# One root chain, modulation ahead of weight splits, and third-tile products one group later in the opening of a two-layer decoder step

## Chip, cores and metric

The kernel runs on one NeuronCore of one Trainium2 chip. The metric is the device time of one execution in microseconds; the times are medians of several executions.

## The reference

One inference step of a two-layer decoder for 512 prompt tokens and 8 sample tokens that share all weights (520 columns in all, width 1024). Each layer computes a modulated norm, a mixer, a gated residual, a second modulated norm, a convolutional feed-forward net and another gated residual. What matters here is the way into the first mixer:

```python
mod = (silu(c) @ w_ada[l] + b_ada[l])[:, None, :]        # c: 1 prompt row, 8 sample rows
sh1, sc1, g1, sh2, sc2, g2 = split(mod, 6, axis=-1)
h = x * rsqrt(mean(x * x, -1, keepdims=True) + 1e-6) * (1 + sc1) + sh1
z = h @ w_in                                             # layer 0: u, v_a, q, k, v
```

Everything is float32.

## The kernel before

Activations lie with the width on the partitions: X is 8 tiles (k = 0 to 7) of 128 partitions and 520 tokens. Every large product is made of three passes in a rounded float32 format: a weight tile W is split into a high part wh (ScalarE, L228) and a low part wl = W - wh (VectorE, L229), the activation h into HH and HL, and the output sums wh·HH, wh·HL and wl·HH. The helper `mm3` issues these three, each for two column ranges (256 and 264), so one weight tile and one k cost six matmuls (rows of L267).

Instructions are issued in the order of the program, each engine's queue in that order; a tile's readers wait for its writers through semaphores. Weight tiles come in the fixed order `stream` (first a query, a key and a value tile of the first mixer) through three raw buffers on SyncE's queue; `issue_load` starts a transfer, `issue_split` makes wh and wl of the next tile, and `weights()` hands out the next pair, splitting it if that is still to be done, and creates background tasks that run at later ticks of `proj`.

The opening (L1205 on) computes the first modulated norm and the first three weight tiles together. The adaLN shift and scale of layer 0 are made in four groups of two k each (`START`), by the generator `h_start(g)`, which `step(g)` moves on to its next `yield`:

- first call: the products of adaLN tiles k = 0 to 3 (L359, 32 matmuls, "ada"); their weights are 8 transfers of 256 KB for a group, issued by `ada_load_start` (L344);
- second call: those of k = 4 to 7, and the evacuation to `adae` on ScalarE (L365);
- third call: the fold product `adat` (L368), which brings shift and scale onto the partitions; then VectorE adds the bias ("mod"), and for each of the group's two tiles makes nt = X·(1 + scale)·rsb; ScalarE makes HH = nt + shift (L1239), VectorE HL = (nt + shift) - HH (L95); some short instructions do the sample columns.

`rsb` holds the reciprocal root of each token's mean square on all partitions. It comes from `rstd_half`, run once for each half of the tokens: sum products with a column of ones (L468), square root on ScalarE (L469), reciprocal on VectorE (L472), a broadcast transpose on TensorE (L477) and a copy (L1256).

The three accumulators are `trip`: query and key in two wide PSUM tiles ("mm"), the value tile in two narrow ones ("tr"). `part(i, k)` is the six matmuls of tile i and k; `qk_part(k)` is those of tiles 0 and 1, a pair; `v_part(g)` is tile 2 for the two k of group g. What sets the order is the list of calls that the diff shows: before, pair 0, then for each group its adaLN halves with pairs between, the fold product, and third-tile products. After the three tiles comes `mixer_even`, whose first product is the next value tile.

Two matmuls on zeros (`warm2`, L1263) stand ahead of pair 0.

Of the kernel before, what the change touches and what calls it, by code (L numbers as in the profile page):

```python
# [8 lines left out]
F32 = mybir.dt.float32  # L9
F32R = mybir.dt.float32r  # L10
AF = mybir.ActivationFunctionType
ALU = mybir.AluOpType
# [3 lines left out]
D = 1024  # L16
KD = 8
TP = 512
NS = 8
T = TP + NS  # L20
# [9 lines left out]
HALF = ((0, H0), (H0, T))  # L30
# [20 lines left out]
def kernel(ctx: ExitStack, tc: tile.TileContext, I: dict, O: dict):  # L51
    nc = tc.nc
    cp = ctx.enter_context(tc.tile_pool(name="cp", bufs=1))
# [20 lines left out]
    def nm(s):  # L74
        uid[0] += 1
        return f"{s}_{uid[0]}"

    def slot(s, dt=F32):
        return bp.tile([128, T], dt, name=nm(s), tag="b")

    def bank(s="ps"):
        return psum["ps"].tile([128, 512], F32, name=nm(s), tag="ps")
# [7 lines left out]
    act, vec, pool, pe = nc.scalar, nc.vector, nc.gpsimd, nc.tensor  # L90
# [3 lines left out]
    def stt(out, in0, s, in1, op0, op1):  # L94
        vec.scalar_tensor_tensor(out, in0, s, in1, op0=op0, op1=op1)  # L95
# [9 lines left out]
    def spawn(gen, delay=0):  # L105
        t = Task(gen, delay)
        tasks.append(t)
        return t
# [35 lines left out]
    ident = cp.tile([128, 128], F32, name="ident")  # L144
    ones = cp.tile([128, 1], F32, name="ones")
    eps = cp.tile([128, 1], F32, name="eps")
# [56 lines left out]
    def issue_load():  # L203
        i = pos["ld"]
        if i >= len(stream):
            return
        ap, n = src(stream[i])
        t = wp.tile([128, 1024], F32, name=nm("wr"), tag="wr", bufs=RBUFS)
        ld(t[:, :n * 128], ap)
        W[i] = (t, n)  # L210
        pos["ld"] += 1
        if stream[i][0] in ("up", "down") and i % 2 == 0 and pos["cp"] < len(copies):
            o, s = copies[pos["cp"]]
            ld(o, s)
            pos["cp"] += 1

    def issue_split():
        i = pos["sp"]
        if i >= len(stream):
            return  # L220
        t, n = W.pop(i)
        if stream[i][0] == "gates":
            h, l = (wp.tile([128, 1024], F32R, name=nm("wa"), tag="wa", bufs=4) for _ in range(2))
        else:
            h = wp.tile([128, 1024], F32R, name=nm("wh"), tag="wh", bufs=WBUFS)
            l = wp.tile([128, 1024], F32R, name=nm("wl"), tag="wl", bufs=WBUFS)
        w = n * 128
        act.activation(h[:, :w], t[:, :w], AF.Copy)  # L228
        vec.tensor_tensor(l[:, :w], t[:, :w], h[:, :w].bitcast(F32), op=ALU.subtract)  # L229
        SPLIT[i] = (h, l)  # L230
        pos["sp"] += 1

    def split_task(i):
        yield 1
        fill_loads()
        while i >= pos["rel"] + WBUFS or pos["sp"] < i or (stream[i][0] == "gates" and not ada_rest.done):
            yield 1
        if pos["sp"] <= i:
            issue_split()
        fill_loads()  # L240
# [5 lines left out]
    def used(n):  # L246
        pos["rel"] += n

    def weights():
        i = pos["use"]  # L250
        while pos["ld"] <= i:
            issue_load()
        while pos["sp"] <= i:
            issue_split()
        pos["use"] += 1
        pos["plan"] = max(pos["plan"], pos["sp"])
        while pos["plan"] <= min(i + SPLIT_AHEAD, len(stream) - 1):
            spawn(split_task(pos["plan"]))
            pos["plan"] += 1
        return SPLIT.pop(i)  # L260
# [92 lines left out]
    def ada_start(g):  # L353
        ts = ada_q.pop(0)
        js, n = START[g], len(START[g])
        ps = bank("ada")
        for k in range(KD):
            for c in range(2 * n):
                pe.matmul(ps[32 * c:32 * c + 32, 0:128], cpad[:, k, :], ts[k][:, 128 * c:128 * c + 128],  # L359
                          start=k == 0, stop=k == KD - 1)  # L360
            if k == 3:
                yield
        r = 64 * n
        ev = sp.tile([128, 512], F32, name=nm("adae"), tag="adae", bufs=1)
        act.activation(ev[0:r, 0:128], ps[0:r, 0:128], AF.Copy)  # L365
        yield
        pt = bank("adat")
        pe.matmul(pt[:, 0:18 * n], ev[0:r, 0:128], fold[0:r, 0:18 * n], start=True, stop=True)  # L368
        ptv = pt[:, 0:18 * n].rearrange("p (c r) -> p c r", c=2 * n)
        for v in (1, 0):  # L370
            s = slice(js[0], js[-1] + 1)
            mod_add(MOD[0][:, v, s, :], ptv[:, v * n:v * n + n, :], 0, v, s)
# [67 lines left out]
    ssq_t = {}  # L440

    def ssq(k, t0=0, t1=T):

        ssq_add()
        if k == 0:
            ssq_t["t"] = slot("ssq")
        t = ssq_t["t"]
        q = t if k == 0 else slot("sq")
        act.activation(q[:, t0:t1], X[:, k, t0:t1], AF.Square)  # L449
        if k:  # L450
            ssq_t["late"] = (t[:, t0:t1], q[:, t0:t1])

    def ssq_add():
        late = ssq_t.pop("late", None)
        if late is not None:
            vec.tensor_tensor(late[0], late[0], late[1], op=ALU.add)

    def rstd_half(half, d1, d2, work=None):

        t = ssq_t["t"]  # L460
        ssq_add()
        yield d1
        ps = bank("ssq")
        starts = [HALF[half][0], HALF[half][0] + 128] + ([T - 128] if half else [])
        n = len(starts)
        sd = sp.tile([128, 4], F32, name=nm("sd"), tag="sd")
        for c, o in enumerate(starts):
            pe.matmul(ps[:, c:c + 1], t[:, o:o + 128], ones, start=True, stop=True)  # L468
        act.activation(sd[:, 0:n], ps[:, 0:n], AF.Sqrt, bias=eps, scale=1.0 / D)  # L469
        if work is not None:  # L470
            work()
        vec.reciprocal(sd[:, 0:n], sd[:, 0:n])  # L472
        yield d2
        rb = bank("rb")
        for c, o in enumerate(starts):
            o -= HALF[half][0]
            pe.transpose(rb[:, o:o + 128], sd[:, c:c + 1].to_broadcast([128, 128]), ident)  # L477
        return rb
# [738 lines left out]
    act_preload(AF.Sqrt)  # L1217
    for k in range(KD):
        ssq(k)

    def run(gen):
        try:
            while True:
                next(gen)
        except StopIteration as e:
            return e.value

    rsb = slot("rsb")

    def h_start(g):  # L1230
        yield from ada_start(g)
        js = slice(START[g][0], START[g][-1] + 1)
        t8 = h_sample_scale(0, 0, js)
        M, c = MOD[0], slice(0, TP)
        ts = []
        for n, k in enumerate(START[g]):
            t = slot("nt")
            stt(t[:, c], X[:, k, c], M[:, 1, k, 0:1], rsb[:, c], ALU.mult, ALU.mult)
            act.activation(HH[:, k, c], t[:, c], AF.Identity, bias=M[:, 0, k, 0:1])  # L1239
            if n == 0:  # L1240
                low = h_sample(0, 0, t8, rsb[:, 256:T], js)
            ts.append((k, t))
        for n, (k, t) in enumerate(ts):
            stt(HL[:, k, c], t[:, c], M[:, 0, k, 0:1], HH[:, k, c].bitcast(F32), ALU.add, ALU.subtract)
            if n == 0:
                low()
# [3 lines left out]
    def step(g):  # L1250
        next(hs[g], None)

    step(0)
    for h, (a, b) in enumerate(HALF):
        r = run(rstd_half(h, 0, 0))
        vec.tensor_copy(rsb[:, a:b], r[:, 0:b - a])  # L1256
    ws = [weights()]
    step(0)
    ws.append(weights())
    step(0)  # L1260
    wps = bank("warm2")
    for _ in range(2):
        pe.matmul(wps, warm[:, 0:128], warm, start=True, stop=True)  # L1263
# [3 lines left out]
    def part(i, k):  # L1267
        mm3(regs[i], ws[i][0], ws[i][1], k, Hs[0][k], Hs[1][k], k == 0, k == KD - 1)

    def qk_part(k):  # L1270
        part(0, k)
        part(1, k)

    def v_part(g):
        part(2, 2 * g)
        part(2, 2 * g + 1)

    qk_part(0)
    ada_load_start(3)
    step(1)  # L1280
    qk_part(1)
    ws.append(weights())
    step(1)
    step(1)
    v_part(0)
    for g in (1, 2):
        step(g + 1)
        qk_part(2 * g)
        step(g + 1)
        qk_part(2 * g + 1)  # L1290
        if g == 2:
            ld(pk[:, PACK["b_ada"][1]:], I["pack"][:, PACK["b_ada"][1]:])
            for _ in range(2):
                issue_load()
        step(g + 1)
        v_part(g)
    issue_split()
    for k in (6, 7):
        qk_part(k)
        part(2, k)  # L1300
    used(3)

    def norm_of(l, which):
# [7 lines left out]
    t = mixer_even(trip_regions, norm_of(0, 1))  # L1311
# [7 lines left out]
    t = ffn(0, after(t), norm_of(1, 0), gate_weights)  # L1319
    t = mixer_odd(after(t), norm_of(1, 1))  # L1320
# [24 lines left out]
    t = ffn(1, after(t), final)  # L1345
    finish(t)
    while pos["cp"] < len(copies):
        o, s = copies[pos["cp"]]
# [128 lines left out]
```

## Time and profile before

| | |
|---|---|
| time, median of 3 runs | 1279.53 us (1277.06 to 1281.1) |
| profiled execution | 1275.57 us |
| its span, first to last instruction | 1273.8 us |
| mean granted TensorE clock | 0.989 |
| TensorE matmul busy | 1236.5 us, 97% |
| VectorE, ScalarE, GpSimd busy | 56%, 45%, 6% |

The times of the trace count from the start of the span. PE is TensorE, DVE is VectorE, ACT is ScalarE, SPq the queue of SyncE that issues transfers. A matmul's end is modelled, so one row may overlap the next. "Idle before" is the time that the engine stood still ahead of an instruction, with what ended it.

### The profile page before, as it was taken

Reading aid. Unit: us, or ns where it says so; the run is one execution under the profiler, and the core shown is the slowest. Engines: PE = TensorE matmul, PEld = TensorE weight load, DVE = VectorE, ACT = ScalarE, POOL = GpSimd, SP = SyncE. Lnnn points to the kernel's source line nnn. Section 1 sums busy time; section 2 is a strip of 40 time slices with the busy share of each in tenths; the row PEclk is TensorE's granted clock in tenths of the full one; section 3 lists DMA queues with packets and bytes.
Section 4 is the critical chain, followed back from the end, with each engine's and each line's share of the span. In section 5 each row is a group of like instructions: output and inputs, shape, how many; then the busy total and the mean of one; then the engine's idle time right before and its main releaser. Section 6 shows DMA issues by size and latency. Waiting matters only on the chain.

```text
span 1273.8 us, 24556 instructions
## 1 busy us (share of the span) xinstructions
PE 1236.5 (97%) x10395; PEld 1159.0 (91%) x10395; DVE 717.7 (56%) x1385; ACT 577.4 (45%) x1002; POOL 79.8 (6%) x143
## 2 busy tenths in 40 slices
PE   8999999999999999999999898999999999999997
PEld 5888767798999999999999898998999999999996
DVE  5646557457743555425664877656655555445544
ACT  4434453235531444214453577734642454225434
POOL 0111322201011000010000000000000000000000
PEclk8999999999999999999999999999999999999998
DMA  9643676755688676775454222245447455545322
GB/s 359 246 162 120 206 249 211 271 182 201 240 275 313 232 261 250 259 255 197 151 204 149 84 84 69 61 142 180 149 162 252 149 199 182 199 153 195 120 81 75
DMA packets 54990, 239.76 MB, mean 188 GB/s; under 512 B 7504, under 2 KB 10328, under 8 KB 53856
## 3 DMA queue, kind: packets, MB, share of 16 engines
q1 hardware_dynamic: 36976, 177.37, 40.3%
q0 software_dynamic: 16816, 59.75, 13.5%
q8 instruction: 82, 1.34, 0.4%
q10 hardware_dynamic: 1088, 1.07, 0.3%
q14 instruction: 28, 0.23, 0.1%
HBM read 232.92 MB, written 72.31 MB: 240 GB/s over the span
## 4 chain that ended last, share of the span: by engine, by line
PE 83%; DVE 5%; ACT 5%; issue 4%; DMA 2%; POOL 1%; SPq 0%; DVEq 0%; POOLq 0%; ACTq 0%
PE mm L267 70%; PE half L267 5%; PE ada L421 2%; ACT wh L228 1%; DVE wl L229 1%; DMA wa<-in_wada 1%; DVE nt L95 1%; DVE HL L95 1%; PE pv L749 1%; PE qk L716 1%; PE ada L388 1%; PE pt L737 1%; DMA X<-in_xT 1%; PE ss L814 0%; DMA wr<-in_w 0%
## 5 line engine op out<-in xcount | busy, mean ns | idle before, releaser
L267 PE MATMUL mm<-HH,wh 128*128 128x256 f32 (+1 forms) x1968 | 420.6, 289 | 7.6 <-DVE X L531 7.3
L267 PE MATMUL mm<-HL,wh 128*128 128x256 f32 (+1 forms) x1968 | 411.5, 284 | 0.7 <-DVE HL L95 0.3
L267 PE MATMUL mm<-HH,wl 128*128 128x256 f32 (+1 forms) x1968 | 409.6, 283 | 0.0
L267 PEld LDWEIGHTS mm<-HH,wh 128*128 128x128 f32 x1968 | 310.7, 189 | 35.8 <-issue 21.2
L267 PEld LDWEIGHTS mm<-HL,wh 128*128 128x128 f32 x1968 | 311.6, 189 | 2.3 <-DVE HL L95 1.9
L267 PEld LDWEIGHTS mm<-HH,wl 128*128 128x128 f32 x1968 | 311.7, 189 | 0.0
L229 DVE TENSOR_TENSOR wl<-wr,wh 128x1024 fp32r<-128x1024 f32 (+1 forms) x188 | 224.3, 1199 | 78.1 <-ACT wh L228 77.1
L228 ACT ACTIVATE wh<-wr 128x1024 fp32r<-128x1024 f32 (+1 forms) x188 | 193.2, 1036 | 111.7 <-PE mm L267 103.5
L95 DVE SCALAR_TENSOR_TENSOR fy<-fraw,pk,fy 128x511 f32<-128x511 f32 (+1 forms) x176 | 132.1, 751 | 190.8 <-ACT fy L604 187.7
L603 ACT ACTIVATE fraw<-mm 128x520 f32<-128x520 f32 x88 | 53.2, 604 | 212.6 <-PE mm L267 212.6
L267 PE MATMUL mm<-gh,wh 128*128 128x256 f32 x576 | 116.8, 284 | 0.0
L267 PE MATMUL mm<-gh,wl 128*128 128x256 f32 x576 | 115.9, 283 | 0.0
L267 PE MATMUL mm<-gl,wh 128*128 128x256 f32 x576 | 115.9, 283 | 0.0
L267 PEld LDWEIGHTS mm<-gh,wh 128*128 128x128 f32 x576 | 89.2, 188 | 7.5 <-issue 7.5
L267 PEld LDWEIGHTS mm<-gh,wl 128*128 128x128 f32 x576 | 89.3, 188 | 0.0
L267 PEld LDWEIGHTS mm<-gl,wh 128*128 128x128 f32 x576 | 89.3, 188 | 0.0
L528 DVE TENSOR_TENSOR r<-mm,mod 128x8 f32<-128x8 f32 x48 | 8.0, 167 | 125.7 <-PE mm L267 125.7
L604 ACT ACTIVATE fy<-mm,pk 128x520 f32<-128x520 f32 x88 | 68.7, 781 | 0.0
L583 ACT ACTIVATE gh<-fs 128x520 fp32r<-128x520 f32 x44 | 28.1, 639 | 81.3 <-DVE fs L621 81.3
L376 POOL DMA_DIRECT2D wa<-in_wada x80 | 42.4, 533 | 335.0 <-PE ada L421 221.9
L449 ACT ACTIVATE sq<-X 128x520 f32<-128x520 f32 (+2 forms) x51 | 25.1, 501 | 76.1 <-DVE X L531 52.9
L584 DVE TENSOR_TENSOR gl<-fs,gh 128x520 fp32r<-128x520 f32 x44 | 30.8, 701 | 30.4 <-ACT gh L583 30.3
(280 smaller groups left out, 1473.5 us busy)
## 6 DMA issues: line engine op xcount, KB each, us to landing
wr<-in_w SPq DMA_DIRECT2D x140, 512.0 KB, 3.7
wa<-in_wada POOLq DMA_DIRECT2D x80, 512.0 KB, 5.7
wr<-in_wd SPq DMA_DIRECT2D x32, 512.0 KB, 3.7
wa<-in_wada SPq DMA_DIRECT2D x32, 256.0 KB, 5.4
out_ck<-in_ck SPq DMA_DIRECT2D x8, 1022.0 KB, 6.6
out_cv<-in_cv SPq DMA_DIRECT2D x8, 1022.0 KB, 6.3
sg<-in_kg POOLq DMA_DIRECT2D x16, 384.0 KB, 4.1
sg<-in_vg POOLq DMA_DIRECT2D x12, 512.0 KB, 5.3
```

Source lines behind the costliest of these rows:

```text
L95: vec.scalar_tensor_tensor(out, in0, s, in1, op0=op0, op1=op1)
L228: act.activation(h[:, :w], t[:, :w], AF.Copy)
L229: vec.tensor_tensor(l[:, :w], t[:, :w], h[:, :w].bitcast(F32), op=ALU.subtract)
L267: pe.matmul(o, w[:, c], x[:, t], start=start and n == 0, stop=stop and n == 2)
L376: st(t, I["wada"][n, k])
L388: pe.matmul(ps[32 * c:32 * c + 32, 0:256], cpad[:, k, :], t[:, 256 * c:256 * c + 256], start=k == 0, stop=k == KD - 1)
L421: pe.matmul(ps[c:c + 32, :], cpad[:, k, :], t[:, 512 * h:512 * h + 512], start=k == 0, stop=k == KD - 1)
L449: act.activation(q[:, t0:t1], X[:, k, t0:t1], AF.Square)
L583: act.activation(h, v, AF.Copy)
L584: vec.tensor_tensor(l, v, h.bitcast(F32), op=ALU.subtract)
L603: act.activation(raw, whole(ps), AF.Copy)
L604: act.activation(y, whole(ps), AF.Identity, bias=b[:, f:f + 1], scale=w[:, 2, f:f + 1])
```

## The change

Four edits, all in the opening:

- The sums of squares of all tokens go through one square root (`sd0`, five columns of 128 tokens) and one reciprocal, then five transposes, one copy of 512 columns and one of 8, in place of two chains over halves. The sum products stand between the two halves of group 0's adaLN products, the transposes behind the second half.
- For group 0, `h_start` has one more `yield` between HH and HL. The first weight's high part is issued ahead of the fold product's modulation, its low part (`q_low`) between HH and HL; the second weight's split follows HL.
- The third weight is taken (`ws.append(weights())`) after group 1's modulation in place of before it.
- The loop now runs over groups n = 1 to 3 (g = n - 1 in the code): first adaLN half of group n, from n = 2 on the third-tile products of group n - 2, pair 2n - 1, second adaLN half, fold product and modulation, pair 2n. The third-tile products of groups 2 and 3 and pair 7 follow the loop.

```diff
--- before.py
+++ after.py
@@ -214,7 +214,10 @@
             ld(o, s)
             pos["cp"] += 1
 
-    def issue_split():
+    def low(t, h, l, w):
+        vec.tensor_tensor(l[:, :w], t[:, :w], h[:, :w].bitcast(F32), op=ALU.subtract)
+
+    def issue_split(low_later=False):
         i = pos["sp"]
         if i >= len(stream):
             return
@@ -226,9 +229,11 @@
             l = wp.tile([128, 1024], F32R, name=nm("wl"), tag="wl", bufs=WBUFS)
         w = n * 128
         act.activation(h[:, :w], t[:, :w], AF.Copy)
-        vec.tensor_tensor(l[:, :w], t[:, :w], h[:, :w].bitcast(F32), op=ALU.subtract)
         SPLIT[i] = (h, l)
         pos["sp"] += 1
+        if low_later:
+            return lambda: low(t, h, l, w)
+        low(t, h, l, w)
 
     def split_task(i):
         yield 1
@@ -1217,13 +1222,9 @@
     act_preload(AF.Sqrt)
     for k in range(KD):
         ssq(k)
-
-    def run(gen):
-        try:
-            while True:
-                next(gen)
-        except StopIteration as e:
-            return e.value
+    ssq_add()
+    blocks = [0, 128, 256, 384, T - 128]
+    sd0 = cp.tile([128, 5], F32, name="sd0")
 
     rsb = slot("rsb")
 
@@ -1240,6 +1241,8 @@
             if n == 0:
                 low = h_sample(0, 0, t8, rsb[:, 256:T], js)
             ts.append((k, t))
+        if g == 0:
+            yield
         for n, (k, t) in enumerate(ts):
             stt(HL[:, k, c], t[:, c], M[:, 0, k, 0:1], HH[:, k, c].bitcast(F32), ALU.add, ALU.subtract)
             if n == 0:
@@ -1251,13 +1254,23 @@
         next(hs[g], None)
 
     step(0)
-    for h, (a, b) in enumerate(HALF):
-        r = run(rstd_half(h, 0, 0))
-        vec.tensor_copy(rsb[:, a:b], r[:, 0:b - a])
-    ws = [weights()]
+    pss = bank("ssq")
+    for c, o in enumerate(blocks):
+        pe.matmul(pss[:, c:c + 1], ssq_t["t"][:, o:o + 128], ones, start=True, stop=True)
+    act.activation(sd0, pss[:, 0:5], AF.Sqrt, bias=eps, scale=1.0 / D)
+    vec.reciprocal(sd0, sd0)
     step(0)
-    ws.append(weights())
+    rb, rb8 = bank("rb"), bank("rb8")
+    for c in range(5):
+        pe.transpose(rb[:, 128 * c:128 * c + 128] if c < 4 else rb8[:, 0:128], sd0[:, c:c + 1].to_broadcast([128, 128]), ident)
+    vec.tensor_copy(rsb[:, 0:TP], rb)
+    vec.tensor_copy(rsb[:, TP:T], rb8[:, 128 - NS:128])
+    q_low = issue_split(True)
     step(0)
+    q_low()
+    step(0)
+    issue_split()
+    ws = [weights() for _ in range(2)]
     wps = bank("warm2")
     for _ in range(2):
         pe.matmul(wps, warm[:, 0:128], warm, start=True, stop=True)
@@ -1277,27 +1290,24 @@
 
     qk_part(0)
     ada_load_start(3)
-    step(1)
-    qk_part(1)
-    ws.append(weights())
-    step(1)
-    step(1)
-    v_part(0)
-    for g in (1, 2):
+    for g in range(3):
         step(g + 1)
-        qk_part(2 * g)
+        if g:
+            v_part(g - 1)
+        qk_part(2 * g + 1)
         step(g + 1)
-        qk_part(2 * g + 1)
         if g == 2:
             ld(pk[:, PACK["b_ada"][1]:], I["pack"][:, PACK["b_ada"][1]:])
             for _ in range(2):
                 issue_load()
         step(g + 1)
-        v_part(g)
+        if g == 0:
+            ws.append(weights())
+        qk_part(2 * g + 2)
+    v_part(2)
     issue_split()
-    for k in (6, 7):
-        qk_part(k)
-        part(2, k)
+    qk_part(7)
+    v_part(3)
     used(3)
 
     def norm_of(l, which):
```

## Rows read from the trace of the kernel before

**Rows 1.** The page: span, busy time and share of each engine.

```profile
span 1273.8 us, 24556 instructions
...
PE 1236.5 (97%) x10395; PEld 1159.0 (91%) x10395; DVE 717.7 (56%) x1385; ACT 577.4 (45%) x1002; POOL 79.8 (6%) x143
```

**Rows 2.** Chain of waits, 8 to 52 us: start, length, what.

```profile
10.37 0.43 SPq L344
...
24.26 1.01 PE ada L359 x32
...
28.77 1.52 PE tr L267 x12
...
31.30 1.69 PE mm L267 x12
...
42.68 0.16 PE adat L368 x2
...
45.58 1.47 PE mm L267 x10
...
49.96 1.44 PE mm L267 x12
```

**Rows 3.** Timeline of the opening: start us, length us, instructions [idle before].

```profile
13.99 0.73 PE L468 MATMUL ssq<-ones,ssq 128*128 128x1 f32 x6
...
15.28 0.54 PE L477 MATMUL rb<-ident,sd 128*128 128x128 f32 x3 [0.56 <-DVE sd L472]
...
15.75 1.35 PE L359 MATMUL ada<-wa,cpad 128*32 128x128 f32 x32
15.86 0.43 DVE L1256 COPY rsb<-rb 128x264 f32<-128x264 f32 x1 [0.63 <-PE rb L477]
...
17.26 2.52 DVE L229 TENSOR_TENSOR wl<-wr,wh 128x1024 fp32r<-128x1024 f32 x2 [0.97 <-ACT wh L228]
...
19.70 0.25 DVE L95 SCALAR_TENSOR_TENSOR mod<-adat,pk 128x18 f32<-128x18 f32 x2
...
20.77 0.72 ACT L1239 ACTIVATE HH<-nt,mod 128x512 fp32r<-128x512 f32 x1 [2.25 <-DVE nt L95]
...
22.49 0.75 DVE L95 SCALAR_TENSOR_TENSOR HL<-nt,mod,HH 128x512 fp32r<-128x512 f32 x1
```

**Rows 4.** DMA issues between 10.36 and 10.8 us, median us to landing.

```profile
wa<-in_wada SPq DMA_DIRECT2D x1, 256.0 KB, 4.5
```

**Rows 5.** Timeline of group 1: start us, length us, instructions [idle before].

```profile
26.52 1.22 DVE L229 TENSOR_TENSOR wl<-wr,wh 128x1024 fp32r<-128x1024 f32 x1 [3.28 <-ACT wh L228]
...
28.36 0.41 PE L368 MATMUL adat<-fold,adae 128*128 128x36 f32 x2 [0.46 <-ACT adae L365]
...
29.89 0.72 ACT L1239 ACTIVATE HH<-nt,mod 128x512 fp32r<-128x512 f32 x1 [1.58 <-DVE nt L95]
...
30.73 0.75 DVE L95 SCALAR_TENSOR_TENSOR HL<-nt,mod,HH 128x512 fp32r<-128x512 f32 x1
```

**Rows 6.** Timeline of TensorE in the last group.

```profile
44.72 0.52 PE L267 MATMUL mm<-HH,wh 128*128 128x256 f32 x2 [0.37 <-ACT HH L1239]
45.58 0.51 PE L267 MATMUL mm<-HL,wh 128*128 128x256 f32 x2 [0.35 <-DVE HL L95]
```

**Rows 7.** Windows: us, busy by engine, granted TensorE clock, DMA share, GB/s.

```profile
core 0: us, PE busy (x) PEld busy (x) DVE busy (x) ACT busy (x) POOL busy (x), PEclk, DMA share, GB/s
16.40:23.10 6.70, 6.26 (x27) 3.04 (x20) 5.69 (x12) 3.64 (x6) 0.00 (x0) 0.50 1.04 392
284.16:286.58 2.42, 0.00 (x1) 0.03 (x1) 2.42 (x9) 1.43 (x4) 0.00 (x0) 0.90 1.56 620
286.50:289.50 3.00, 2.92 (x14) 2.95 (x15) 2.51 (x9) 1.55 (x4) 0.00 (x0) 0.50 0.03 5
708.46:714.00 5.54, 3.12 (x27) 3.15 (x27) 4.85 (x16) 3.15 (x7) 0.00 (x0) 1.00 0.20 81
```

**Rows 8.** Waits of TensorE: total us, times, longest.

```profile
PE ada L388 <- DMA wa<-in_wada: 1.2, 3, 0.6
```

## The prediction

> **What bounds the kernel.** I read the page first: TensorE is busy 97% of 1273.8 us, so whatever holds it back anywhere reaches the end, unless a later wait takes it up [rows 1]. The change touches only the first 50 us, so all that counts is when TensorE leaves the opening: in the chain of waits, the product after the three tiles starts at 49.96 [rows 2]. That chain changes its character shortly before 24.26, where the first adaLN product of group 1 starts: ahead of it the limits are transfers and VectorE, behind it TensorE almost without a break. The timeline then tells what each step waits for.
>
> Up to 24.26 the reader is to see three things. The last adaLN tile of group 0 is issued at 10.37 and lands 4.5 us later, at 14.87, while the second half of that group's products starts only at 15.75, behind the second root chain [rows 2 to 4]. VectorE works without a pause from 17.26: two low parts of weights, then the modulation from 19.70 to the end of the second low part of the activations, at 22.49 + 0.75 = 23.24 [rows 3]. And the granted clock is 0.50, or 1.2 GHz, from 16.40 to 23.10 [rows 7].
>
> From 24.26 to 49.96 every group has the same blocks: two adaLN halves, two query/key pairs, the fold product (adat), third-tile products. What matters is what stands between the fold product and the first pair that needs its group. The fold product of group 1 ends at 28.77; its modulated tile HH is finished at 29.89 + 0.72 = 30.61 and its low part HL at 31.48 [rows 5]. Before, TensorE fills that time with third-tile products (1.52) and the next adaLN half (1.0), and the pair starts at 31.30 without a wait [rows 2]. Only in the last group, where one cover is missing, does it stand still: 0.37 us for HH and 0.35 for HL [rows 6].
>
> **The change, part by part.**
>
> *One root chain.* Removed: one square root, one reciprocal and the return trip between the engines. The five sum products and five transposes stay. Ten sum instructions, at 0.73 for six, are 1.2 us and lie ahead of the landing at 14.87, as do root and reciprocal. So the second adaLN half is now set by the landing: 14.87 plus a quarter of 1.35 is 15.2. Transposes: 5/3 of 0.54 is 0.9, to 16.1 [rows 3, 4]. The two copies of the row factors, 0.43 each, become a wide one and a short one, an operation that the trace doesn't show; between one such copy and two I put the two at 0.87, as before. They start after the fourth transpose, at 15.95, so the modulation can start at 16.8 instead of 19.70. The fold product follows the transposes and is ready by then.
>
> *Modulation ahead of the splits.* Those 2.9 us do not reach TensorE whole. The two low parts of weights, 1.25 each, move from in front of the modulation to the inside and the end of it. VectorE still does all of it before the first pair is complete, for the pair's last products read the second tile's low weights. Sum: 16.8 + 3.54 (from 19.70 to 23.24) + 2.5 = 22.8; two last products of some 0.4 end at 23.2 or 23.3, against 24.26. Gain 1.0 us. The weights are there in time: the high part of the first was ready at 17.26 [rows 3]. Bounds: at best TensorE waits for nothing but the first HH, 1.79 after the modulation starts (19.70 to 20.77 + 0.72), so 18.6, plus a pair of 1.69: 20.3, a gain of 4.0. At worst the clock is still low when VectorE is done; three microseconds more at half rate cost 1.5, a loss of 0.5. I take 1.0, because the rows give VectorE no idle time to lose.
>
> *Loop order.* Here the change adds a wait. Pair 2g+2 now stands right behind the fold product and the modulation that makes its operands. The third-tile products that lay there come a group later, behind the next adaLN half, where nothing waits. So TensorE, whose rows stand in program order, meets in each of three groups:
> - the evacuation of the adaLN sums, 0.46 (group 1 has it before too; the others had a pair in between) [rows 5];
> - the fold product alone instead of in the stream, 0.41 against 0.16, so 0.25 [rows 2, 5];
> - fold product to HH: 28.77 to 30.61, and in the last group 42.84 to 44.72. I take 1.90;
> - HH to HL: the 0.35 that the last group shows [rows 6].
>
> Together 2.96, three times 8.9. Before, the same kinds sum to 0.46 + 0.25 + 0.37 + 0.35 = 1.4. The loss is 7.5 us. Queued behind the waiting pair are the next adaLN half and the third-tile products, ready but not reached. Bounds: if the wait for HL hides in all three, 7.5 - 0.7 = 6.8; if every restart fills the pipeline anew, as a pair behind an adaLN half does (1.69 against 1.52 for twelve products in the stream), 8.0.
>
> *What moves at no cost.* The third weight's split now runs behind group 1's modulation. There VectorE ends the second tile's HL some 3.5 after the fold product (31.48 + 0.75 less 28.77), and the low weights 1.22 later, near 4.7. Third-tile products start at 1.90 + 0.86 + 1.47 for the pair and 1.0 for the adaLN half, that is 5.2, and read the low weights last; if that cover goes, the split's lateness is paid. No DMA is reordered: the three weight loads are issued already, and the tasks that the moved calls create run only at later ticks. SyncE's adaLN loads pass no new wait, and TensorE asks for groups 2 and 3 later than before. The fourth split keeps third-tile products, a pair and third-tile products behind it, three times 1.5 us or so, against 1.22 on VectorE and about as long on ScalarE.
>
> *Clock.* The new waits leave TensorE mostly idle for 3 us in each group. The trace has five gaps of 2.0 to 2.4 us later on. After three (at 284, 823, 876) the granted clock fell to 0.50 for about 3 us; after two (708, 714) it stayed at 1.00 [rows 7]. A fall costs half of 3.0 us of bound work, 1.5. The new gaps are a little shorter and broken by a few products, so I count a fall in each as somewhat below one in two and take one of three; bounds none and three, 0 to 4.5. [...]
>
> **Sum.** -1.0 + 7.5 + 1.5 = +8.0 us. The profiled execution took 1275.57 (span 1273.8 and 1.8 around it), which would become 1283.6. It lies 4.0 below the median of the runs, 1279.53; carried to the median the forecast is **1287.5 us**.
>
> Could a later wait absorb it? TensorE's later waits go back to VectorE and ScalarE, which shift along. Only 1.2 us of them are for adaLN transfers [rows 8], so at most that comes back; I take nothing off.
>
> **Rivals.**
> 1. *The clock falls in every group.* Place: the pairs and adaLN products behind each wait. For: three of five gaps. Against: the last group before stood still twice within a microsecond at full clock. Time: 6.5 + 4.5 = +11.0, or 1290.5; with two falls 1289.0.
> 2. *The opening pays at its bound.* If the waits for low parts don't bind, TensorE gains 4.0 instead of 1.0: -4.0 + 7.5 = +3.5, or 1283.0, within the 0.3% (3.8 us) that a measurement here can tell from no change. Against it: VectorE's unbroken work up to the low weights.
> 3. *Faster: TensorE does not stand still.* If it takes ready products from behind a waiting one, each new wait is filled, the old ones too, and the opening as well, since group 1's first adaLN half is ready behind pair 0: -4.0 - 1.4 = -5.4, or 1274.1. It decides as soon as less than 0.8 us of wait per group remains (1.0 + 1.4, over three). Against it: before the fold product at 28.36 TensorE waited 0.46 for the evacuation, although the third-tile products behind it had their last operand, the low weights, at 26.52 + 1.22 = 27.74 [rows 5].
>
> **Chances.** The forecast, with no fall or one: 0.48. Two or three falls: 0.37. Opening at its bound: 0.09. No standing still: 0.06. The range for 8 in 10 leaves out rival 3 and the ends of the others: 1282.0 to 1292.5, from no fall (1286.0) with the opening near its bound to three falls with the spread of the runs (2 us either way) on top. Faster by over 0.3%: 0.04; within: 0.10; slower: 0.86. Rival 3 gives 0.04 to faster and 0.02 to within, rival 2 some 0.08 to within.
>
> **What would show it.** Right: in front of pairs 2, 4 and 6, behind the fold products, TensorE idles about 1.9 us until ScalarE's HH and then 0.3 until HL; group 1's first adaLN product starts near 23.3; VectorE begins the modulation near 16.8 and ends the second low weights near 22.8; the product after the three tiles starts some 8 us later than 49.96. Wrong: third-tile products in those gaps; group 1's first adaLN product near 20; waits for DMA in front of adaLN products; a stage that ends late and a span that doesn't.

## The result and the profile after

The changed kernel takes 1286.88 us (median of 5 executions, 1285.86 to 1290.19) against 1278.07 for the kernel before (median of 5, 1276.69 to 1281.1). The ratio is 1.0073, with an interval of 1.005 to 1.0095: 9 us slower, where +8.0 was forecast. The profiled execution is the slowest of the five, 1290.19 us, so its trace shows more loss than the median has.

The page of the changed kernel, its span and the busy times, which answer to [rows 1]:

```profile
span 1288.4 us, 24554 instructions
...
PE 1243.5 (97%) x10395; PEld 1166.6 (91%) x10395; DVE 717.1 (56%) x1384; ACT 576.8 (45%) x1001; POOL 79.5 (6%) x143
```

The span is 14.6 us longer; the instructions of TensorE are as many as before. VectorE's and ScalarE's work is unchanged, so the difference is waiting and pace. The chain of waits of the changed kernel, start, length and what, in the places of [rows 2]:

```profile
23.04 1.01 PE ada L364 x32
...
30.33 2.43 PE mm L272 x10
32.76 1.57 PE ada L364 x32
...
61.87 1.45 PE mm L272 x12
```

Group 1's first adaLN product starts at 23.04 (24.26 before): the opening gained 1.2 us. The product after the three tiles starts at 61.87 (49.96 before): from one to the other it is 38.83 us where it was 25.70. The timeline of the opening tells where the 1.2 come from (start, length, instruction, idle before), next to [rows 3, 4]:

```profile
15.08 0.43 PE L364 MATMUL ada<-wa,cpad 128*32 128x128 f32 x8 [0.25 <-DMA wa<-in_wada]
...
16.12 0.69 DVE L1266 COPY rsb<-rb 128x512 f32<-128x512 f32 x1 [1.60 <-PE rb L1265]
...
16.81 0.25 DVE L95 SCALAR_TENSOR_TENSOR mod<-adat,pk 128x18 f32<-128x18 f32 x2
...
18.66 0.50 PE L272 MATMUL mm<-HH,wh 128*128 128x256 f32 x2 [0.52 <-ACT HH L1240]
...
20.66 0.51 PE L272 MATMUL mm<-HL,wh 128*128 128x256 f32 x2 [1.50 <-DVE HL L95]
...
21.26 1.22 DVE L218 TENSOR_TENSOR wl<-wr,wh 128x1024 fp32r<-128x1024 f32 x1
...
22.54 0.50 PE L272 MATMUL mm<-HH,wl 128*128 128x256 f32 x2 [0.66 <-DVE wl L218]
```

The second adaLN half ends on the last tile's landing (15.08, waiting for DMA). The wide copy takes 0.69, the modulation starts at 16.81 and the second low weights end at 21.26 + 1.22 = 22.48; TensorE waits for them at 22.54. The pair stands three times, for 0.52, 1.50 and 0.66 us, and still ends earlier than before. Now the rows behind the fold products, TensorE alone, which answer to [rows 5, 6]:

```profile
27.15 0.41 PE L373 MATMUL adat<-fold,adae 128*128 128x36 f32 x2 [0.46 <-ACT adae L370]
29.46 0.51 PE L272 MATMUL mm<-HH,wh 128*128 128x256 f32 x2 [1.89 <-ACT HH L1240]
30.33 0.70 PE L272 MATMUL mm<-HL,wh 128*128 128x256 f32 x2 [0.36 <-DVE HL L95]
```

Evacuation 0.46, HH 1.89, HL 0.36: the three waits of the prediction. Groups 2 and 3 show the same (0.46, 1.90; 0.46, 1.90, 0.36), except that HL is not waited for in group 2, where the products of HH run at half the clock. That is the fourth item, seen in the windows from 23 to 62 us (length, busy time of each engine, granted clock, DMA), next to [rows 7]:

```profile
core 0: us, PE busy (x) PEld busy (x) DVE busy (x) ACT busy (x) POOL busy (x), PEclk, DMA share, GB/s
23.00:30.48 7.48, 4.77 (x82) 3.84 (x82) 2.80 (x10) 1.94 (x5) 0.00 (x0) 1.00 1.05 391
30.48:33.88 3.40, 3.40 (x34) 3.09 (x38) 1.90 (x2) 0.84 (x1) 0.00 (x0) 0.50 1.06 396
33.88:40.72 6.84, 4.94 (x74) 4.22 (x66) 1.37 (x7) 0.60 (x2) 0.00 (x0) 1.00 0.98 371
40.72:47.54 6.82, 6.30 (x49) 5.29 (x50) 2.10 (x4) 1.23 (x3) 0.00 (x0) 0.50 0.04 14
47.54:54.38 6.84, 4.44 (x57) 3.71 (x55) 2.38 (x8) 1.47 (x4) 0.00 (x0) 1.00 0.00 0
54.38:57.78 3.40, 3.09 (x14) 3.09 (x15) 3.06 (x6) 1.30 (x2) 0.00 (x0) 0.50 0.00 0
57.78:62.00 4.22, 4.22 (x37) 4.22 (x37) 1.36 (x5) 2.21 (x4) 0.20 (x1) 1.00 0.41 124
```

At each of the three waits the clock falls to 0.50, that is 1.2 GHz, once for 6.8 us (from 40.72, still within the wait, which ends at 41.18) and twice for 3.4 behind the wait, with TensorE busy nearly throughout; in the chain, ten products of pair 2 take 2.43 at 30.33 in place of 1.47, and the adaLN half behind them 1.57 in place of 1.01. Before, the same stage ran at full clock: 1.00 from 24 to 50 us.

### The profile page after: what moved, and what is told of

It reads as the page before. It is cut to its first block, busy times and chain, and to the rows that moved or that the text cites. A ratio compares the mean times of both kernels' runs of the same rounds, so it can differ in the third digit from the quotient of the medians.

```text
span 1288.4 us, 24554 instructions
## 1 busy us (share of the span) xinstructions
PE 1243.5 (97%) x10395; PEld 1166.6 (91%) x10395; DVE 717.1 (56%) x1384; ACT 576.8 (45%) x1001; POOL 79.5 (6%) x143
## 4 chain that ended last, share of the span: by engine, by line
PE 83%; DVE 6%; ACT 5%; issue 4%; DMA 2%; POOL 1%; SPq 0%; DVEq 0%; POOLq 0%; ACTq 0%
PE mm L272 70%; PE half L272 5%; PE ada L426 2%; DVE wl L218 1%; ACT wh L231 1%; DMA wa<-in_wada 1%; DVE nt L95 1%; DVE HL L95 1%; PE pv L754 1%; PE qk L721 1%; PE ada L393 1%; PE ada L364 1%; PE pt L742 1%; PE tr L272 1%; DMA X<-in_xT 1%
```

## Experiments

All times are medians beside the kernel before on the same chip (1278.77 us in 21 executions for e1 to e4, 1279.31 in 17 for e5 to e7, 1277.97 in one for e8). A ratio and its interval are estimated from the single executions; the difference in us behind a ratio is worked out from it, and can lie 1 us or so from the difference of the medians. "The stage" is from group 1's first adaLN product to the first product after the three tiles, in the chain of waits: 25.70 us before, 38.83 in the changed kernel.

### e1: the loop order alone

```diff
     qk_part(0)                       # opening as before
     ada_load_start(3)
-    step(1); qk_part(1); ws.append(weights()); step(1); step(1); v_part(0)
-    for g in (1, 2): ...
+    for g in range(3): ...           # the changed kernel's loop
```

> The kernel before with the new loop order alone; the opening up to pair 0 is the old one. Theory (the waits in front of pairs 2, 4 and 6 are the loss): group 1's first adaLN product starts at 24.2 to 24.3 as before, then three waits of about 1.9 us for HH and 0.35 for HL, the product after the three tiles 7.5 us later than 49.96 plus 1.7 for each fall of the granted clock; time 7.5 to 12.6 us over before. Rival (the loss comes from the new opening or from the third weight's later split): within 2 us of before.

Measured: 1291.01 us, ratio 1.0085 (1.0061 to 1.0108), 11 us slower. Its timeline has the waits, its windows two falls of the clock behind them, and its chain a late end of the stage:

```profile
30.65 0.41 PE L368 MATMUL adat<-fold,adae 128*128 128x36 f32 x2 [0.46 <-ACT adae L365]
32.96 0.50 PE L267 MATMUL mm<-HH,wh 128*128 128x256 f32 x2 [1.90 <-ACT HH L1239]
```

```profile
34.50:37.90 3.40, 3.40 (x40) 2.69 (x39) 1.37 (x2) 0.31 (x1) 0.00 (x0) 0.50 1.03 401
...
44.76:48.16 3.40, 3.28 (x16) 2.75 (x20) 1.55 (x4) 0.72 (x1) 0.00 (x0) 0.50 0.00 0
48.16:62.60 14.44, 11.73 (x139) 10.80 (x136) 6.79 (x17) 4.81 (x9) 0.02 (x1) 1.00 0.12 37
```

```profile
25.47 1.87 PE ada L359 x32
...
62.65 1.44 PE mm L267 x12
```

So the loop order alone makes a loss as large as the whole change; the rival falls. Behind group 3's wait, of the same 1.90 us, the clock stayed up. The old opening of this execution was itself 1.2 us late (25.47 in place of 24.26): the first weight landed later, the evacuation of group 0 stood behind its split on ScalarE, and the fold product waited 1.40 for it. The clock also fell for 3.4 us from 24.3, behind a wait of 1.89 in pair 0, which is why the first adaLN half takes 1.87; that part of the stage's 37.18 us doesn't belong to the new waits.

### e2 and e8: the opening alone

```diff
-    for g in range(3): ...           # the changed kernel's loop
+    step(1); qk_part(1); ws.append(weights()); step(1); step(1); v_part(0)
+    for g in (1, 2): ...             # as before
```

> The changed kernel with the loop order of before: only the root chain, the modulation ahead of the splits, and the first two weights' splits are new. Theory: group 1's first adaLN product starts near 23.0 instead of 24.2, only the last group's 0.7 us of waits is left, the clock doesn't fall behind it, the product after the three tiles starts 1.2 us before 49.96; time 1 us under before, not to be told from no change. Rival: some of the 9 us stays, because the new opening itself holds VectorE or a transfer up.

> The opening's edits with the loop order of before, once more, for a second profile. Theory (the clock's fall behind pair 0 in the first profile comes in some executions and costs 1.5 us): without the fall the product after the three tiles starts near 23.2 + 25.7 = 48.9, 1 us before 49.96. Rival (the fall belongs to the new opening, whose waits in pair 0 always bring it): it falls again near 23 and the stage ends near 50.5.

Measured: e2 1277.18 us, ratio 0.998 (0.9967 to 0.9992): 2.6 us faster, 1.0 to 4.2 (1.6 by the medians), a little more than forecast. Its profiled execution, the slowest of ten at 1279.08, shows a fall of the clock that was not expected, in the first 3.4 us behind pair 0, and a stage of 27.16 us; e8 (1275.79 us, one execution) shows none, and 48.57 - 22.89 = 25.68. The chain of e2, then that of e8:

```profile
23.38 1.86 PE ada L364 x32
25.24 2.31 PE mm L272 x12
...
50.54 1.44 PE mm L272 x12
```

```profile
22.89 1.01 PE ada L364 x32
...
48.57 1.45 PE mm L272 x12
```

In e2 the first adaLN half takes 1.86 and pair 1 2.31, in place of 1.01 and 1.62. So the broken pair 0 can bring a fall, which costs 1.5, and doesn't always; it is not peculiar to the new opening, since e1 shows one with the old. Without it the stage ends at 48.57, 1.4 before 49.96.

### e3: the waits filled with products of zeros

```diff
         if g == 0:
             ws.append(weights())
+        fps = bank("fill")
+        for _ in range(2):
+            pe.matmul(fps, warm[:, 0:128], warm, start=True, stop=True)
         qk_part(2 * g + 2)
```

> The changed kernel with two products of zeros (128 x 512) put into each of the three waits, behind the fold product and ahead of pairs 2, 4 and 6; at full clock four rows of 0.43, some 1.7 us, less than the 1.9 us of the wait. Theory (a wait costs its length, and each fall of the clock behind it 1.7 more): the granted clock stays at 1.00 from 24 to 60, the waits end when they did, the product after the three tiles starts 7.5 - 1.2 = 6.3 us after 49.96, 3 to 5 us earlier than in the profile of the changed kernel; time 5 to 7 us over before. Rival (the clock's falls are hidden in the waits): the clock stays up and the stage ends no earlier than in the changed kernel, near 61.9.

Measured: 1285.37 us, ratio 1.0048 (1.0029 to 1.0066), 6 us slower than before and so less slow than the changed kernel. The timeline of group 1 and the window from 19 to 58:

```profile
28.06 0.41 PE L373 MATMUL adat<-fold,adae 128*128 128x36 f32 x2 [0.46 <-ACT adae L370]
28.30 1.96 PE L1308 MATMUL fill<-warm 128*128 128x512 f32 x4
30.36 0.51 PE L272 MATMUL mm<-HH,wh 128*128 128x256 f32 x2
31.23 0.51 PE L272 MATMUL mm<-HL,wh 128*128 128x256 f32 x2 [0.36 <-DVE HL L95]
```

```profile
19.00:58.00 39.00, 34.12 (x363) 26.35 (x362) 19.61 (x46) 12.35 (x24) 0.67 (x1) 1.00 0.62 233
```

```profile
23.95 1.01 PE ada L364 x32
...
57.40 1.44 PE mm L272 x12
```

From the fold product to the first product of HH it is 2.30 us, as in the changed kernel (29.46 - 27.15 = 2.31), so the fill delays nothing. The clock is 1.00 throughout, and the stage takes 57.40 - 23.95 = 33.45 us. That splits the 38.83 of the changed kernel's profile: the waits cost 33.45 - 25.70 = 7.75, the falls of the clock 38.83 - 33.45 = 5.4. The rival, falls hidden in the waits, is out. The stage ends 7.4 after 49.96 where 6.3 was forecast, because the opening of this execution was later than the changed kernel's, 23.95 against 23.04.

### e4: third-tile products back in the gaps

```diff
-        if g:
-            v_part(g - 1)
...
+        if g == 0:
+            ws.append(weights())
         step(g + 1)
-        if g == 0:
-            ws.append(weights())
+        v_part(g)
         qk_part(2 * g + 2)
...
-    v_part(2)
```

> The changed kernel with the third-tile products of the same group put back between the fold product and pairs 2, 4 and 6 (1.5 us of cover), the rest of the new loop order kept; the third weight is split ahead of group 1's modulation, as before. Theory (a wait costs what its cover lacks): the wait for HH falls from 1.9 to about 0.4 us and that for HL stays at 0.35, so each group loses 1.5 us less, the clock stays up, the product after the three tiles starts 7.5 - 4.5 - 1.2 = 1.8 us after 49.96; time within 3 us of before. Rival (any break in front of a pair, however short, costs the clock): falls to 0.50 remain and the stage ends 5 us or more late.

Measured: 1283.49 us, ratio 1.003 (1.0019 to 1.0042), 4 us slower than before. The waits of TensorE from 12 to 62 us (total, times, longest) and the window:

```profile
PE adat L373 <- ACT adae L370: 1.4, 3, 0.5
PE mm L272 <- ACT HH L1240: 1.3, 3, 0.5
...
PE tr L272 <- ACT wh L231: 0.5, 1, 0.5
PE tr L272 <- DVE wl L218: 0.5, 1, 0.5
```

```profile
55.01 1.45 PE mm L272 x12
```

```profile
19.00:55.00 36.00, 29.10 (x347) 24.08 (x346) 19.41 (x47) 11.93 (x22) 0.04 (x1) 1.00 0.68 249
```

The waits for HH shrink to 0.49, 0.39 and 0.39, as forecast, and no fall follows: here breaks of half a microsecond left the clock at 1.00. The size was missed: the stage ends 5.0 after 49.96 where 1.8 was forecast, and the time is some 4 us over before where at most 3 was. The third weight's split, moved in front of the modulation, came late for the products meant as cover, with two new waits of 0.5 us for wh and wl; VectorE made that low part first and began group 1's modulation at 30.46, 1.7 after the fold product's end. The opening ended at 24.3 in this execution, so the gain of 1.2 was missing too.

### e5: the root chain alone

```diff
-    q_low = issue_split(True)
+    ws = [weights() for _ in range(2)]
     step(0)
-    q_low()
     step(0)
-    issue_split()
-    ws = [weights() for _ in range(2)]
```

This is e2 with the first two splits ahead of the modulation again.

> The opening's one root chain alone: the first two weights are split ahead of the modulation and the loop has its old order. Theory (VectorE sets the opening, and the modulation's place decides): the modulation still starts behind the second low weights, near 19.7, group 1's first adaLN product at 24.2 as before, a gain of nothing. Rival (the chain itself sets it): group 1's first adaLN product near 23.0.

Measured: 1279.09 us, one execution, beside 1279.31. The timeline of VectorE and TensorE:

```profile
15.91 0.69 DVE L1266 COPY rsb<-rb 128x512 f32<-128x512 f32 x1 [1.60 <-PE rb L1265]
...
17.21 2.47 DVE L218 TENSOR_TENSOR wl<-wr,wh 128x1024 fp32r<-128x1024 f32 x2 [0.53 <-ACT wh L231]
...
19.60 0.25 DVE L95 SCALAR_TENSOR_TENSOR mod<-adat,pk 128x18 f32<-128x18 f32 x2
...
21.45 0.51 PE L272 MATMUL mm<-HH,wh 128*128 128x256 f32 x2 [3.52 <-ACT HH L1240]
```

The row factors are ready at 16.7, and VectorE then does both low parts first; the modulation starts at 19.60, against 19.70 before, and TensorE stands 3.5 us. Group 1's first adaLN product starts at 24.58. In this one execution the one chain by itself gains nothing, as far as the clock lets it be seen: it fell behind that wait too, from about 22.7.

### e6: the same products in another order

```diff
+    ada_load_start(3)
+    step(1); part(0, 0); part(0, 1); part(1, 0); step(1); part(1, 1); step(1)
+    step(2); ws.append(weights()); qk_part(2); step(2); part(0, 3); step(2)
+    part(1, 3); v_part(0)
+    step(3); qk_part(4); step(3); part(0, 5)
+    ...                              # two weight loads, as before
+    step(3); part(1, 5); v_part(1); part(2, 4)
+    qk_part(6); issue_split(); part(2, 5); qk_part(7); v_part(3)
```

> The new opening with another order of the same products: group 1's first adaLN half goes ahead of pair 0; then every fold product has products behind it that don't need its group (the next adaLN half, the other half of a pair, third-tile products), and every adaLN evacuation half a pair. Theory (only the waits count; the work is the same): no wait over 0.5 us for HH between 24 and the end of the stage, the clock stays up, the product after the three tiles starts near 46.5, 3 us before 49.96; time 2 to 4 us under before. Rival (transfers bind once the waits are gone): waits for adaLN tiles appear and the stage ends near 49 to 50.

Measured: 1274.76 us, ratio 0.996 (0.9947 to 0.9974): 5 us faster than before, 3.3 to 6.8, the fastest of all. Its waits of TensorE from 12 to 62 us are one line; the window and the chain's end follow:

```profile
PE ada L364 <- DMA wa<-in_wada: 1.8, 7, 0.5
```

```profile
19.00:47.40 28.40, 27.18 (x347) 23.33 (x346) 19.26 (x44) 11.67 (x22) 0.07 (x1) 1.00 0.86 320
```

```profile
47.39 1.44 PE mm L272 x12
```

No wait for HH, HL or an evacuation is left and the clock stays up. Both theories have a share: the 1.8 us that remain are seven waits for adaLN tiles, four of them (1.1 us) in group 2's first half, which now comes before its transfers. The stage ends at 47.39, 2.6 before 49.96. The rest of the 5 us isn't seen in the opening: the profiled execution of before, at 1275.57, is 3.7 under the median of before on this chip, while e6's, at 1274.38, is near its own, so the profiles stand closer together than the medians; which later part makes it was not followed up.

### e7: the changed kernel once more

> The changed kernel once more, for a second profile. Theory (the falls of the clock behind the waits vary from one execution to the next): the waits in front of pairs 2, 4 and 6 are again 1.9 and 0.35 us, to 0.1; the loss of clock in the stage differs from the first profile's 6.8 us by steps of 1.7. Rival: the falls are fixed by the program and come at the same three places for the same length.

Measured: 1291.97 us, one execution, beside 1279.31. Its windows:

```profile
32.40:35.80 3.40, 3.40 (x41) 2.69 (x41) 1.28 (x2) 0.21 (x1) 0.00 (x0) 0.53 1.05 405
...
42.84:46.24 3.40, 3.06 (x23) 2.65 (x25) 1.27 (x3) 0.53 (x1) 0.00 (x0) 0.50 0.00 0
...
53.00:60.00 7.00, 6.03 (x26) 5.73 (x27) 4.72 (x10) 2.50 (x4) 0.00 (x0) 0.51 0.24 70
```

The waits are again 1.89 or 1.90 us and the clock falls at all three. The sum of the falls is the same as in the first profile, against the theory (13.6 us at the half rate, which is the expectation's 6.8 us if TensorE had had work throughout; e3 gives 5.4); but the long one is now the last, not the second, against the rival. The product after the three tiles starts at 62.85; the opening ended 1.3 us later than in the first profile, behind a wait of 1.05 for an adaLN tile.

## Why the prediction was right, step by step

**What bounds the stage.** Right: every wait added in front of TensorE reached the stage's end (e3: 7.75 us of waits, nothing taken up before 57.40).

**One root chain, modulation ahead of the splits.** Right in both steps: landing, copies (0.85 against 0.87), modulation at 16.81 (16.8 forecast), second low weights at 22.48 (22.8), gain 1.2 (1.0). The size is that of one profile against one, and it varies: with the same opening, group 1's first adaLN product starts at 22.89 in e8, 23.38 in e2, 23.95 in e3 and about 24.3 in e4 and e7. In the last three the clock was at 0.50 for 3.4 us from about 15, with the transposes in it, and at 1.00 there in the others; the sum had no term for that. That the opening as a whole gains is shown by e2's time. The reading that the chain alone doesn't count rests on e5, one execution. A fall of the clock behind the broken pair 0, which comes near the prediction's lower bound, came in e2 and not in e8 or the changed kernel.

**Loop order.** Right, and shown by e1 and e3: three sets of waits, forecast 7.5, measured 7.75. The third weight's split was covered as forecast; e4, where it isn't, shows the price of a lost cover.

**Clock.** The mechanism was right and the size too small. The term was one fall of 1.5 us out of three. In three profiles with the new loop (the changed kernel, e7, e1) eight of nine waits brought a fall, of 3.4 or 6.8 us, and in the changed kernel's profile they cost 5.4. The step that failed is the count, "somewhat below one in two", taken from the five gaps before; that the new gaps are broken by a few products didn't protect them. The count also left out a sixth gap of the trace before, 3.9 us up to 778.2, at whose end the clock fell too. What tells a wait that is followed by a fall from one that isn't (group 3 of e1) stays open.

The Trainium skill ("TensorE: Matmul & The Clock Gate", section "HAM oscillation — how this bites in real kernels") tells of a kernel in which the clock fell back at every tile, where each wait for a transfer was longer than the burst of matmuls ahead of it. Here waits of 1.90 us, much shorter than the work between them, brought falls as well.

**Sum.** For the profiled execution: -1.2 + 7.75 + 5.4 = +11.9 at the stage's end, as read (61.87 - 49.96). It must come out so, since the terms are differences of the same stages; what tests the prediction is each term by itself. The other 2.7 of the 14.6 us of span come later, from code that didn't change, and they are a net figure. First some of the delay comes back: the product that starts at 710.88 before starts at 721.05, 10.2 later. Behind it lies a window in which the clock was 1.00 before (the end of 708 to 714 in [rows 7] and what follows):

```profile
725.70:732.60 6.90, 6.08 (x29) 6.09 (x30) 3.46 (x10) 1.03 (x3) 0.00 (x0) 0.58 0.49 152
```

The product behind the next wait (778.18 before) starts 12.8 later, so this fall cost 2.7 us. Such falls after the later gaps differ from one execution to the next. The waits for adaLN transfers took up 0.9 us (1.2 in [rows 8], 0.3 after); but 1.7 in all came back between the stage's end and 711, more than the prediction's bound of 1.2. Where the other 0.8 came from was not followed up.

The medians differ by 8.8 us (9.3 by the ratio, 6.4 to 12.1), while the two profiles of the changed kernel show +11.9 and about +13 at the stage's end. Two more numbers bear on what the falls cost in the median. e3, whose profile has no fall behind its waits, is 6.1 us over before by its ratio (3.7 to 8.4), 3.2 under the changed kernel, on another chip and with overlapping intervals. And the mean granted clock of an execution, of which 0.001 is some 2.6 us at the half rate, was 0.982 in the changed kernel's profiled execution and 0.984 to 0.986 in the other four (0.980 in e7), and 0.989 in the profiled execution of before, against 0.986 on average in 21 others. So this pair of profiles has more of a difference in the clock than the medians have. How often all three falls come in executions without a profile was not measured; the term's size in the median stays open between the 1.5 forecast and 5.4, and the near hit of 1287.5 on 1286.88 is partly luck in this term.

**Rivals.** All three falls (rival 1) is what both profiles of the changed kernel show, though not the median time (1290.5 by that rival). TensorE never took a ready product past a waiting one: e4's and the changed kernel's gaps are empty (rival 3). The opening did not come near its bound of 4.0 (rival 2). e6 shows what that bound was made of: with group 1's first adaLN half ahead of pair 0, the waits for low parts vanish.

## What to carry to other kernels

Behind every product whose result goes through another engine and comes back, put work that needs neither, as long as the round trip (here 2.8 us to HL); one block of 1.5 us taken away costs the block (a wait for HH of 1.90 in place of 0.39 in e4) and can cost the clock on top. Moving a chain earlier pays only as far as the engine that runs it has slack: in the changed kernel's profile the modulation came 2.9 us earlier and 1.2 arrived. A gap that can't be covered can be filled with products of zeros; in e3 that brought back the clock's part of the loss and nothing of the waits.

## What was not expected of the hardware

In these traces falls of the granted clock came in two lengths, 3.4 and 6.8 us, whatever the work behind the wait (the low stretch at the very end of a program apart), and TensorE was busy through most of them. Equal waits of 1.90 us were followed by 3.4, by 6.8 or by nothing (group 3 of e1). Breaks of up to 0.5 us, three to five per group in e4, brought none. A long wait isn't the only thing that goes before a fall, though: in the openings of e3, e4 and e6 the clock fell for 3.4 us from about 15, with TensorE at work in nearly all of the 2 us before, and no wait over 0.61, 0.94 and 0.33 us since its first products on zeros ended, near 10.2. What else brings one stays open.
